# Dense second stage of a PEER layer: gating held one pair of columns ahead, weight tiles of the first stage recorded with priority

## The chip, the cores and the metric

The program runs on one core of a Trainium2 chip. The metric is the device time of one execution in microseconds (us), lower is better. PE is the matrix engine, DVE the vector engine, ACT the scalar engine, POOL the engine that issues indirect gathers, SP the queue that issues all other transfers.

## What is computed

Two stacks of layers follow each other in one program. The change lies in the first stack, in the feed-forward part of its two layers, which picks 128 of 16384 experts for each token and adds their outputs. Cut to what matters:

```python
def peer_ffn(h, wq, subkeys, u, v):
    ...                                   # scores, two top-16, cand, top-16 of cand
    gate = jax.nn.softmax(top, axis=-1)
    def block(args):
        hk, ek, gk = args
        act = jax.nn.gelu(jnp.einsum('ted,td->te', u[ek], hk), approximate=False)
        return jnp.einsum('te,ted->td', gk * act, v[ek])
```

The second stack (fox, gla, gdn and gated feed-forward layers) is not touched.

## The kernel before

`peer` (from L909) runs once in each of the two layers, `l` = 0 and 1. Layer 0 has 512 tokens: 128 of them fetch their experts by gathers (`fetched`, L895 and L900 on DVE, L899 on POOL), the other 384 take the dense way. In layer 1 all 256 tokens are dense. The dense way multiplies every token with every expert and lets the gates, zero for most, choose. The 16384 experts are 128 columns of 128.

The first stage makes the activations. `ahead` (L968) takes one column: `load_w` (L277) loads its weights (`wraw`, 512 KB), ACT rounds them into `whi` (L217), DVE takes the rest into `wlo` (L284), PE runs 24 matmuls (L982), ACT applies gelu into `ev`, and every second column a store puts two columns into the DRAM tensor `u` (L987). Beside it `route` works out the gates: top-16 searches on DVE (`choose`), then `spread`, whose step makes one-hot rows of four tokens (`oa` L836, `ob` L845 in layer 1), multiplies them (PE, L849), and ACT lays the result out for a store into the DRAM tensor `g` (L855). Columns are called from between the steps of `route` by a plan of costs (`tp`, `td`); what is left runs behind it.

The second stage goes over the 128 columns in pairs. `load_u` (L1019) brings four columns of `u` into a tile `ad`, `load_g` (L1012) eight columns of `g` into `gt`, `load_v` (L1024) one column's value rows into `vr`. `gated` (L1029) multiplies a pair's activations by its gates (two DVE multiplications, L1038) and splits the product into `wt`: the rounded half on ACT, the rest on DVE (L294). `products` (L1042) splits a column's `vr` into `whi` (ACT) and `wlo` (DVE, L294) and runs its matmuls (L1054): 18 in layer 0, 12 in layer 1, the last third of which need `wlo`. Buffers: two for `ad`, two for `gt`, three for `wt`, five (layer 0) or six (layer 1) for `vr`, two for `wlo` in layer 0 and three in layer 1.

The program writes the instructions down in the order of the Python code; a scheduler at build time then orders each engine's queue by priority (earlier written comes first, unless raised by `high_priority`), by when it thinks data and buffers are there, and by edges that the kernel adds itself. One such edge is made by `behind` (L204): it puts an instruction behind the last one noted in `self.last` for its engine, which for DVE is the last rest-half of `load_w` or `split` that was written down. Each engine then runs its queue in that fixed order.

Of the kernel before, what the change touches and what calls it, by code (L numbers as in the profile page):

```python
# [52 lines left out]
         dict(nbig=2048, bufs=0, w=(6, 0, 0), mm=2, sm=6, sp=6, uv=4, H=1, acc=1))  # L53
ROUTE = (dict(bufs=7, rt=1, VI=1, t=3, r=13, alt=1, oa=3, ob=2, ev=2),
         dict(bufs=5, rt=1, VI=1, t=3, r=13, alt=2, oa=3, ob=2, ev=4, xw=1, whi=2, wlo=2))
DENSE = (dict(bufs=0, gt=2, ad=2, wt=3, vr=5, o=2, jk=1), dict(bufs=0, gt=2, ad=2, wt=3, vr=6, whi=3, wlo=3, o=2))

LAST = 8
KEEP = dict(xhl=2, nq=3, na=1, nr=2)
WORK2 = (dict(bufs=3, tn=L2, t=14, er=1, g0=2, qg=1, kl=8, hh=16, qs=8, vn=4, p=4, pT=4, o=9, mm=3, sm=1, S=2, PT=1, PO=1),  # L60
         dict(bufs=7, tn=L2, t=7, m=6, at=4, lv=2, o=6, y=5, mm=2, sm=1, A=5),
         dict(bufs=6, tn=L2, t=4, p=3, ce=5, el=1, mt=1, lq=4, DT=4, DTm=1, NL=4, NLm=1, XT=4, XTm=1, aT=4, aTm=1, dl=5,
              o=4, r=6, mm=2, sm=2, A=4),
# [23 lines left out]
class Kern:  # L87
# [171 lines left out]
    def t(self, n=None, dt=F32, tag="t"):  # L259
        if tag in KEEP:  # L260
            return self.keep.tile([P, n or self.tn], dt, name=tag, bufs=KEEP[tag])
        pool = self.lower_tmp if tag in self.lower_tags else self.tmp
        return pool.tile([P, n or self.tn], dt, name=tag, bufs=self.tags[tag])
# [645 lines left out]
    def peer(self, l, extra=()):  # L909
        nc, A, x = self.nc, self.A, self.x  # L910
# [32 lines left out]
        def fetch_for(us, every):  # L943

            nonlocal fd
            n = 0
            if steps:
                fd += us
                while fd >= every:
                    fd -= every  # L950
                    n += next(steps[0], 1) is None
            return n
# [15 lines left out]
        def ahead():  # L968
            nonlocal early
            j = early  # L970
            early += 1
            ps = self.ps("MM")[:, :ND]
            if whole:
                raw = self.w.tile([P, 1024], F32, name="wraw", bufs=self.wb[0])
                nc.sync.dma_start(raw, A["uT"][l, j])
                terms = [(raw[:, k * P:(k + 1) * P], xw[:, k]) for k in range(KD)]
            else:
                hi, lo = self.load_w(A["uT"][l, j])
                terms = [(hi[:, k * P:(k + 1) * P], z[k, dc]) for k in range(KD) for z in (xh, xl)]
                terms += [(lo[:, k * P:(k + 1) * P], xh[k, dc]) for k in range(KD)]  # L980
            for i, (w_, x_) in enumerate(terms):
                nc.tensor.matmul(ps, w_, x_, start=i == 0, stop=i == len(terms) - 1)  # L982
            if j % 2 == 0:
                pair.append(self.t(2 * ND, tag="ev").rearrange("p (j t) -> p j t", j=2))
            self.last["ACT"] = self.actv(pair[-1][:, j % 2], ps, AF.Gelu).ins
            if j % 2:
                nc.sync.dma_start(U[:, j - 1:j + 1], pair.pop())  # L987

        done = 0
        for pe, dve in self.route(l, xh, xl, cs, G, F, fetch):  # L990
            n = fetch_for(dve, EVERY[l])
            done += n
            tp, td = tp + pe, td + dve + n * 2.55
            while tp < td and early < P - LAST:
                ahead()
                tp, td = tp + ND * CU[l], td + (0.0 if whole else 1.1)
        while early < P:
            ahead()
            done += fetch_for(ND * CU[l], 10.0)
        routing.close()  # L1000
        self.part(dense, **DENSE[l])
        left = F - done
# [5 lines left out]
        J, JU, JG = 2, 4, 8  # L1008
        gts, ads, raws = {}, {}, {}
        b3 = lambda z: z.rearrange("p (b t) -> p b t", t=GT)  # L1010

        def load_g(n):  # L1012
            if n < P // JG:
                gt = self.t(JG * ND, tag="gt")
                gts[n] = gt.rearrange("p (b j t) -> p j b t", j=JG, t=GT)
                nc.sync.dma_start(gt.rearrange("p (b j) -> p b j", b=nb),
                                  G[:, :nb, n * JG:(n + 1) * JG].rearrange("p b j t -> p b (j t)"))

        def load_u(n):  # L1019
            if n < P // JU:  # L1020
                ads[n] = self.t(JU * ND, tag="ad").rearrange("p (j t) -> p j t", j=JU)
                nc.sync.dma_start(ads[n], U[:, n * JU:(n + 1) * JU])
# [6 lines left out]
        def gated(j0):  # L1029

            if j0 % JG == 0:
                load_g(j0 // JG + 1)
            if j0 % JU == 0:
                load_u(j0 // JU + 1)
            wt = self.t(J * 2 * ND, F32R, "wt").rearrange("p (j s t) -> p j s t", j=J, s=2)
            a = ads[j0 // JU][:, j0 % JU:j0 % JU + J]
            for jj in range(J):
                nc.vector.tensor_mul(b3(a[:, jj]), b3(a[:, jj]), gts[j0 // JG][:, j0 % JG + jj])  # L1038
            self.split(a, wt[:, :, 0], wt[:, :, 1])
            return wt  # L1040

# [23 lines left out]

        VR = DENSE[l]["vr"] - 1
        load_g(0)
        load_u(0)
        for j in range(VR):
            load_v(j)  # L1070
        prev = None
        for j0 in range(0, P, J):
            w = gated(j0)
            if prev is not None:
                products(*prev)
                if j0 % 8:
                    next(extra, None)
                fetch_for(left, P // J - 1)
            prev = (j0, w)
# [30 lines left out]
        for c in range(nd):  # L1110
            o = self.t(D, tag="o")
# [928 lines left out]
```

## Time and profile before

| what | us |
|---|---|
| three runs | 4589.56, 4605.82, 4605.38 |
| their median | 4605.38 |
| the profiled execution | 4596.78 |
| its span, first to last instruction | 4595.0 |
| PE busy in it | 4333.2 (94%) |
| DVE busy | 3382.9 (74%) |
| ACT busy | 2288.5 (50%) |

In that execution the first stage of layer 0 lies between about 387 and 1205 us, its second stage between 1222.7 and 1789.6; the first stage of layer 1 lies between about 2010 and 2558, its second stage between 2569.7 and 2925. Bracketed times in a row of a timeline are the idle time of the engine just before the instruction and what ended it. A busy PE is not a PE at its peak, as its matmuls are pipelined: the number of matmuls in a stretch and the granted clock beside it say more.

### The profile page before, as it was taken

To read this page: it belongs to the slowest core of one execution; us is meant where nothing else is said; L and a number is where in the kernel's file an instruction comes from. 1 tells how busy PE (TensorE), PEld (TensorE's weight loads), DVE (VectorE), ACT (ScalarE), POOL (GpSimd) and SP (SyncE) were. 2 spreads that over 40 slices of the span, in tenths; PEclk is the share of its full clock that TensorE was granted. 3 is DMA by queue.
4 is the path that set the end of the run, shared out by engine and by line. 5 is a ranking of instruction groups with operands and counts; after the bars stand their busy time and mean duration, and the time that the engine had idled before them with its cause. 6 is when DMAs were issued, how large, how long until landed. Compare 5 with 4: busy or idle time off the path is not lost. (4 is left out here: it accounts for less than half of the span.)

```text
span 4595.0 us, 71892 instructions
## 1 busy us (share of the span) xinstructions
PE 4333.2 (94%) x27588; PEld 3934.9 (86%) x27588; DVE 3382.9 (74%) x6338; ACT 2288.5 (50%) x4316; POOL 207.6 (5%) x136
## 2 busy tenths in 40 slices
PE   6999799899899999989999899999999999999999
PEld 5887799899787777889899787779988988899899
DVE  9986998888587667989954566676576576656765
ACT  4443246477333334554544444575445454445753
POOL 0000012222111110000000000000000000000000
PEclk8999899999999999999999999999999998999999
DMA  5423388889898774465577888425544552155355
GB/s 189 133 64 105 113 307 328 318 306 337 306 371 298 277 280 150 146 189 183 195 250 228 273 282 282 140 81 150 173 120 134 172 152 69 52 174 154 92 171 173
DMA packets 262505, 909.39 MB, mean 198 GB/s; under 512 B 26112, under 2 KB 68992, under 8 KB 240016
## 3 DMA queue, kind: packets, MB, share of 16 engines
q1 hardware_dynamic: 243728, 770.57, 51.5%
q0 software_dynamic: 18432, 134.23, 8.0%
q8 instruction: 216, 3.54, 0.3%
q14 instruction: 129, 1.06, 0.1%
HBM read 819.49 MB, written 84.93 MB: 197 GB/s over the span
## 5 line engine op out<-in xcount | busy, mean ns | idle before, releaser
L217 ACT ACTIVATE whi<-wraw 128x1024 fp32r<-128x1024 f32 (+2 forms) x796 | 831.9, 1046 | 995.6 <-PE MM L307 545.7
L284 DVE TENSOR_TENSOR wlo<-wraw,whi 128x1024 fp32r<-128x1024 f32 (+2 forms) x796 | 957.3, 1204 | 289.8 <-ACT whi L217 167.6
L307 PE MATMUL MM<-xhl,whi 128*128 128x272 f32 (+1 forms) x4736 | 938.8, 295 | 6.9 <-ACT whi L217 6.4
L307 PE MATMUL MM<-b,whi 128*128 128x272 f32 (+2 forms) x3712 | 855.7, 324 | 59.2 <-ACT b L217 50.6
L307 PEld LDWEIGHTS MM<-xhl,whi 128*128 128x128 f32 x4736 | 754.7, 191 | 28.1 <-issue 10.3
L307 PEld LDWEIGHTS MM<-b,whi 128*128 128x128 f32 x3712 | 624.5, 193 | 114.4 <-ACT b L217 56.6
L307 PE MATMUL MM<-xhl,wlo 128*128 128x272 f32 (+1 forms) x2368 | 691.2, 292 | 2.2 <-DVE wlo L284 2.1
L982 PE MATMUL MM<-b,whi 128*128 128x384 f32 (+1 forms) x4096 | 676.8, 315 | 7.4 <-ACT ev L217 7.4
L1054 PE MATMUL SM<-whi,wt 128*128 128x512 f32 x2560 | 632.0, 394 | 30.8 <-ACT whi L217 30.5
L982 PEld LDWEIGHTS MM<-b,whi 128*128 128x128 f32 x4096 | 624.8, 193 | 9.7 <-ACT ev L217 8.8
L1054 PEld LDWEIGHTS SM<-whi,wt 128*128 128x128 f32 x2560 | 487.6, 191 | 135.2 <-ACT whi L217 31.6
L307 PE MATMUL MM<-b,wlo 128*128 128x272 f32 (+2 forms) x1856 | 598.4, 324 | 5.2 <-DVE wlo L284 4.6
L307 PEld LDWEIGHTS MM<-xhl,wlo 128*128 128x128 f32 x2368 | 451.6, 191 | 10.2 <-issue 4.7
L217 ACT ACTIVATE whi<-vr 128x1024 fp32r<-128x1024 f32 x256 | 271.0, 1059 | 366.4 <-PE SM L1054 309.1
L307 PEld LDWEIGHTS MM<-b,wlo 128*128 128x128 f32 x1856 | 356.4, 192 | 30.7 <-DVE wlo L284 9.9
L982 PE MATMUL MM<-b,wlo 128*128 128x384 f32 (+1 forms) x2048 | 348.5, 313 | 28.6 <-DVE wlo L284 28.6
L1054 PE MATMUL SM<-wlo,wt 128*128 128x512 f32 x1280 | 342.5, 399 | 27.3 <-DVE wlo L294 27.0
L294 DVE TENSOR_TENSOR wlo<-vr,whi 128x1024 fp32r<-128x1024 f32 x256 | 310.4, 1222 | 65.3 <-ACT whi L217 50.3
L982 PEld LDWEIGHTS MM<-b,wlo 128*128 128x128 f32 x2048 | 314.1, 191 | 33.8 <-DVE wlo L284 33.2
L1054 PEld LDWEIGHTS SM<-wlo,wt 128*128 128x128 f32 x1280 | 243.2, 192 | 86.6 <-DVE wlo L294 36.9
L1038 DVE TENSOR_TENSOR ad<-ad,gt 128x384 f32<-128x384 f32 (+1 forms) x256 | 112.8, 488 | 221.5 <-DMA ad<-u 185.7
L899 POOL DMA_INDIRECT uv<-uv,sp x128 | 206.6, 1614 | 1517.0 <-DVE acc L895 907.6
(473 smaller groups left out, 5125.3 us busy)
## 6 DMA issues: line engine op xcount, KB each, us to landing
wraw<-uT SPq DMA_DIRECT2D x256, 512.0 KB, 4.6
vr<-uv SPq DMA_DIRECT2D x256, 512.0 KB, 7.0
wraw<-w_gate_up SPq DMA_DIRECT2D x176, 512.0 KB, 3.6
g<-b SPq DMA_DIRECT2D x40, 1024.0 KB, 9.0
wraw<-w_in SPq DMA_DIRECT2D x64, 512.0 KB, 3.8
wraw<-fox_w_in SPq DMA_DIRECT2D x64, 512.0 KB, 3.6
wraw<-w_down SPq DMA_DIRECT2D x64, 512.0 KB, 3.5
wmod<-wmodT SPq DMA_DIRECT2D x56, 512.0 KB, 3.8
```

The lines of the kernel that those rows point to most:

```text
L217: r = nc.scalar.activation(out, in_, func, **kw)
L284: self.last["DVE"] = nc.vector.tensor_sub(lo[:, :n], raw[:, :n], hi[:, :n].bitcast(F32)).ins
L294: self.last["DVE"] = self.nc.vector.tensor_sub(lo, src, hi.bitcast(F32)).ins
L307: nc.tensor.matmul(ps, w_, x_[k, slice(a, b)], start=(i == 0 and q == 0), stop=(i == kc - 1 and q == 2))
L899: nc.gpsimd.indirect_dma_start(z, None, self.A[f"uv{l}"], bass.IndirectOffsetOnAxis(ap=ids[:, js], axis=0))
L982: nc.tensor.matmul(ps, w_, x_, start=i == 0, stop=i == len(terms) - 1)
L1038: nc.vector.tensor_mul(b3(a[:, jj]), b3(a[:, jj]), gts[j0 // JG][:, j0 % JG + jj])
L1054: nc.tensor.matmul(res[c][h], wt[:, jj, s_, c * P:(c + 1) * P], v[:, h * 512:(h + 1) * 512], start=first and q == 0 and s_ == 0, stop=end ...
```

## The change

Four edits: the multiplications of `gated` get the edge of `behind`; in layer 1 `ad` gets a third buffer and `load_u` runs two tiles ahead instead of one (two before the loop, in front of the first `vr`); and `load_w` in the first stage is written down with priority, in both layers (both have more than 192 dense tokens).

```diff
-DENSE = (dict(bufs=0, gt=2, ad=2, wt=3, vr=5, o=2, jk=1), dict(bufs=0, gt=2, ad=2, wt=3, vr=6, whi=3, wlo=3, o=2))
+DENSE = (dict(bufs=0, gt=2, ad=2, wt=3, vr=5, o=2, jk=1), dict(bufs=0, gt=2, ad=3, wt=3, vr=6, whi=3, wlo=3, o=2))
...
+AHEAD = (1, 2)
...
-                hi, lo = self.load_w(A["uT"][l, j])
+                with self.tc.high_priority():
+                    hi, lo = self.load_w(A["uT"][l, j])
...
-                load_u(j0 // JU + 1)
+                load_u(j0 // JU + AHEAD[l])
...
-                nc.vector.tensor_mul(b3(a[:, jj]), b3(a[:, jj]), gts[j0 // JG][:, j0 % JG + jj])
+                self.behind(nc.vector.tensor_mul(b3(a[:, jj]), b3(a[:, jj]), gts[j0 // JG][:, j0 % JG + jj]), "DVE")
...
-        load_u(0)
+        for n in range(AHEAD[l]):
+            load_u(n)
```

No instruction is added or taken away on any engine, and the order of POOL stays as it was. Everything behind layer 1's second stage keeps its order. Lines of the changed kernel are two to four higher than those of before.

DVE in layer 0's second stage, around the gating of the tile `ad_13026`. Before:

```order
L294 TENSOR_TENSOR wt_12967<-ad_12788,wt_12967 128x2x384
L895 SCALAR_TENSOR_TENSOR acc_2891<-uv_12961,sp_4381,acc_2891 128x1024
L294 TENSOR_TENSOR wlo_12975<-vr_12856,whi_12974 128x1024
L1038 TENSOR_TENSOR ad_13026<-ad_13026,gt_12904 128x384 x2
L294 TENSOR_TENSOR wlo_12999<-vr_12880,whi_12998 128x1024
L900 SCALAR_TENSOR_TENSOR uv_13020,sp_4380<-uv_13020,H_4341 128x1024
L294 TENSOR_TENSOR wt_13028<-ad_12906,wt_13028 128x2x384
L1038 TENSOR_TENSOR ad_13026<-ad_13026,gt_12904 128x384 x2
L294 TENSOR_TENSOR wlo_13036<-vr_12913,whi_13035 128x1024
```

The same tile in the changed kernel:

```order
L902 SCALAR_TENSOR_TENSOR uv_13020,sp_4380<-uv_13020,H_4341 128x1024
L1041 TENSOR_TENSOR ad_12906<-ad_12906,gt_12666 128x384 x2
L897 SCALAR_TENSOR_TENSOR acc_2891<-uv_13020,sp_4381,acc_2891 128x1024
L296 TENSOR_TENSOR wlo_13036<-vr_12913,whi_13035 128x1024
L296 TENSOR_TENSOR wt_13028<-ad_12906,wt_13028 128x2x384
L296 TENSOR_TENSOR wlo_13060<-vr_12937,whi_13059 128x1024
L1041 TENSOR_TENSOR ad_12906<-ad_12906,gt_12666 128x384 x2
L296 TENSOR_TENSOR wt_13081<-ad_12906,wt_13081 128x2x384
L296 TENSOR_TENSOR wlo_13089<-vr_12972,whi_13088 128x1024
L296 TENSOR_TENSOR wlo_13113<-vr_12996,whi_13112 128x1024
L902 SCALAR_TENSOR_TENSOR uv_13134,sp_4380<-uv_13134,H_4341 128x1024
L1041 TENSOR_TENSOR ad_13026<-ad_13026,gt_12904 128x384 x2
```

The first gating of `ad_13026` stood in front of `wlo_12999`; it now stands behind `wlo_13113`, which is five columns later (12999, 13036, 13060, 13089, 13113). Its buffer is that of `ad_12788`, which is free once `wt_12967` is written. Counted over the 64 pairs of layer 0, a pair's gating stood 5 to 9 columns ahead of the column it belongs to for 55 of them; now it stands 2 columns ahead for 62. In layer 1 it stood 3 to 7 columns ahead for 56 pairs and now stands 2 ahead for 63.

SP at the start of layer 1's second stage. Before:

```order
L1016 DMA gt<-g_66 128x8x256
L1022 DMA ad<-u_68 128x1024
L1027 DMA vr<-uv 128x1024 x5
L1016 DMA gt<-g_66 128x8x256
L1022 DMA ad<-u_68 128x1024
```

In the changed kernel:

```order
L1019 DMA gt<-g_66 128x8x256
L1025 DMA ad<-u_68 128x1024 x2
L1030 DMA vr<-uv 128x1024 x5
L1019 DMA gt<-g_66 128x8x256
L1025 DMA ad<-u_68 128x1024
```

A second tile of `u` (512 KB) is asked for ahead of the five `vr`. From the third tile on, an `ad` load stands nine columns ahead of its gating in the changed layer 1; in the changed layer 0 it stands five columns ahead (counted as above, against the `vr` load in front of it).

DVE at the end of `spread` in layer 1, before:

```order
L845 TENSOR_SCALAR ob<-iotaf,rt 128x128 x4
L836 TENSOR_TENSOR oa<-iotaf,rt 128x512
L845 TENSOR_SCALAR ob<-iotaf,rt 128x128 x4
L284 TENSOR_TENSOR wlo<-wraw,whi 128x1024
L836 TENSOR_TENSOR oa<-iotaf,rt 128x512
L845 TENSOR_SCALAR ob<-iotaf,rt 128x128 x4
L836 TENSOR_TENSOR oa<-iotaf,rt 128x512
L845 TENSOR_SCALAR ob<-iotaf,rt 128x128 x4
L836 TENSOR_TENSOR oa<-iotaf,rt 128x512
L845 TENSOR_SCALAR ob<-iotaf,rt 128x128 x4
L284 TENSOR_TENSOR wlo<-wraw,whi 128x1024 x82
```

In the changed kernel:

```order
L847 TENSOR_SCALAR ob<-iotaf,rt 128x128
L286 TENSOR_TENSOR wlo<-wraw,whi 128x1024
L847 TENSOR_SCALAR ob<-iotaf,rt 128x128 x3
L838 TENSOR_TENSOR oa<-iotaf,rt 128x512
L847 TENSOR_SCALAR ob<-iotaf,rt 128x128 x4
L838 TENSOR_TENSOR oa<-iotaf,rt 128x512
L847 TENSOR_SCALAR ob<-iotaf,rt 128x128 x2
L286 TENSOR_TENSOR wlo<-wraw,whi 128x1024
L847 TENSOR_SCALAR ob<-iotaf,rt 128x128 x2
L838 TENSOR_TENSOR oa<-iotaf,rt 128x512
L847 TENSOR_SCALAR ob<-iotaf,rt 128x128 x4
L286 TENSOR_TENSOR wlo<-wraw,whi 128x1024 x66
```

Weight tiles stood one to five or six steps of `spread` and now stand one to two or three; 16 tiles fewer are left behind it. In layer 0 the number of tiles in front of each landmark of the routing moves by two at most.

## Rows read from the trace of the kernel before

**Rows 1.** Windows, L1054 alone: PE busy (matmuls), weight loads, granted clock, DMA share, GB/s.

```profile
1222.70:1480.00 257.30, 246.16 (x1043) 201.37 (x1044) 0.96 0.92 334
1480.00:1670.00 190.00, 174.95 (x735) 142.11 (x735) 0.95 0.78 275
1670.00:1790.00 120.00, 119.79 (x529) 98.91 (x527) 1.00 0.63 217
2569.70:2925.00 355.30, 353.88 (x1536) 288.45 (x1536) 1.00 0.83 279
```

**Rows 2.** Timeline of PE, layer 0's second stage: start, duration, instructions, [idle before].

```profile
1222.71 5.49 PE L1054 MATMUL SM<-whi,wt 128*128 128x512 f32 x12 [19.23 <-ACT whi L217]
...
1313.09 2.88 PE L1054 MATMUL SM<-whi,wt 128*128 128x512 f32 x12
...
1317.17 2.88 PE L1054 MATMUL SM<-whi,wt 128*128 128x512 f32 x12
...
1789.63 1.95 PE L1091 MATMUL MM<-ident,acc 128*128 128x128 f32 x16
```

**Rows 3.** Waits of PE, 1222 to 1800: us in total, times, longest.

```profile
PE SM L1054 <- DVE wlo L294: 26.2, 10, 4.5
```

**Rows 4.** Timelines of SP, DVE and PE around the longest of these waits.

```profile
1537.68 0.33 SPq L1022 DMA_DIRECT2D ad<-u  x1
...
1550.11 1.03 DVE L1038 TENSOR_TENSOR ad<-ad,gt 128x384 f32<-128x384 f32 x2 [10.12 <-DMA ad<-u]
1551.06 1.22 DVE L294 TENSOR_TENSOR wlo<-vr,whi 128x1024 fp32r<-128x1024 f32 x1
...
1544.91 2.88 PE L1054 MATMUL SM<-whi,wt 128*128 128x512 f32 x12
1552.33 2.86 PE L1054 MATMUL SM<-wlo,wt 128*128 128x512 f32 x6 [4.54 <-DVE wlo L294]
```

**Rows 5.** Waits of DVE, 1222 to 1800.

```profile
DVE ad L1038 <- DMA ad<-u: 87.5, 19, 10.1
```

**Rows 6.** Page, costliest groups: busy, mean ns, then idle before and its releasers.

```profile
L1038 DVE TENSOR_TENSOR ad<-ad,gt 128x384 f32<-128x384 f32 (+1 forms) x256 | 112.8, 488 | 221.5 <-DMA ad<-u 185.7
```

**Rows 7.** Windows, all engines, first stage of layer 1 (the last is its tail).

```profile
2110.00:2222.00 112.00, 107.69 (x872) 105.08 (x870) 111.98 (x237) 57.01 (x89) 0.00 (x0) 1.00 0.61 191
2222.00:2330.00 108.00, 95.20 (x730) 89.69 (x729) 107.20 (x294) 54.35 (x142) 0.00 (x0) 1.00 0.57 212
2330.00:2558.00 228.00, 228.00 (x1902) 228.00 (x1901) 95.60 (x78) 105.11 (x157) 0.00 (x0) 1.00 0.72 224
```

**Rows 8.** Instructions on the tile ad, both layers: transfer, issue to landing.

```profile
DMA to landing us min/median/max: 4.3/8.3/20.8
```

**Rows 9.** Windows, all engines (PE, PEld, DVE, ACT, POOL), layer 0's second stage.

```profile
1260.00:1290.00 30.00, 30.00 (x134) 24.82 (x134) 28.25 (x40) 12.09 (x18) 6.17 (x3) 1.00 1.02 388
1310.00:1400.00 90.00, 90.00 (x399) 74.54 (x398) 75.71 (x102) 35.58 (x48) 12.49 (x8) 1.00 0.93 343
```

**Rows 10.** Timelines of DVE, ACT and PE, start of layer 1's second stage.

```profile
2566.55 1.43 DVE L1038 TENSOR_TENSOR ad<-ad,gt 128x256 f32<-128x256 f32 x4 [12.50 <-DMA ad<-u]
...
2568.61 1.04 ACT L217 ACTIVATE whi<-vr 128x1024 fp32r<-128x1024 f32 x1
...
2569.70 3.63 PE L1054 MATMUL SM<-whi,wt 128*128 128x512 f32 x8 [11.29 <-ACT whi L217]
```

**Rows 11.** Groups by form, 1670 to 1790: the two halves of wt.

```profile
L294 DVE TENSOR_TENSOR wt<-ad,wt 128x768 fp32r<-128x768 f32 x12 | 11.5, 955 | 0.0
...
L217 ACT ACTIVATE wt<-ad 128x768 fp32r<-128x768 f32 x12 | 10.2, 847 | 3.3 <-PE SM L1054 3.3
```

**Rows 12.** Groups by form, 2222 to 2320.

```profile
L284 DVE TENSOR_TENSOR wlo<-wraw,whi 128x1024 fp32r<-128x1024 f32 x10 | 12.6, 1255 | 0.0
```

**Rows 13.** First stage of layer 0: window 387 to 1205, and one PE wait.

```profile
387.00:1205.00 818.00, 756.95 (x4367) 727.54 (x4365) 704.24 (x1467) 442.32 (x1088) 139.97 (x90) 0.96 0.74 268
...
PE MM L880 <- DVE sp L931: 6.8, 1, 6.8
```

## Prediction

> **What bounds the kernel now.** PE is busy for 94% of the span, so I looked for the stretches where it stands still or runs slowly, and asked which of them the edits can reach. I read the windows of the two second stages first, then PE's waits, then the timelines around the longest one, and last the windows of the first stages.
>
> In layer 1's second stage PE is busy for 353.88 of 355.30 us at full clock [rows 1]: nothing to win but its start. Layer 0's second stage is another matter. At full clock one column takes 4.08 us, from 1313.09 to 1317.17 [rows 2], so 128 columns want 522.2 us. From the first matmul at 1222.71 to the first one behind the stage at 1789.63 it took 566.9 [rows 2]: 44.7 too many. PE's waits name 26.2 of them, ten waits for `wlo` [rows 3]. The other 18.5 are matmuls at the lower of the two clock levels behind a wait and small gaps: the granted clock is 0.96 and 0.95 in the first two stretches against 1.00 in the third [rows 1], and after the 4.54 us wait six matmuls took 2.86 us where 1.4 is usual (a third of 4.08) [rows 2, 4].
>
> Why is `wlo` late? Rows 4 show it. SP asks for a tile of `u` at 1537.68; DVE sits idle for 10.12 us until it lands, does the gating at 1550.11 and only then, at 1551.06, the `wlo` that PE has wanted since about 1547.8. That `wlo` needs nothing of the tile; it merely stands behind the gating. DVE lost 87.5 us in 19 such waits in this stage [rows 5]; over both layers `ad` ended 185.7 us of idle time in front of the gating [rows 6].
>
> In the first stage of layer 1 DVE is the bound of `spread`: 107.20 of 108 us busy from 2222 to 2330, while PE has 95.20 [rows 7]. Behind it PE runs alone at full rate, 228.00 of 228 [rows 7].
>
> **The change, term by term.** No instruction comes or goes, so every term is idle PE time, or slow PE time, won or lost.
>
> Gating, layer 0. In the example the tile's gating moves five columns later, behind five `wlo`s. At 4.08 us each the load then has about 20 us from its issue, plus what stood between before, against a landing of 8.3 us in the median and 20.8 at most [rows 8]. So nearly all waits for `ad` leave DVE, and those of PE for `wlo` with them. The hold doesn't delay the load: the buffer is freed by the last `wt` of the tile two earlier, which moves back with its own gating, but so does the use. What can be won is 44.7 less the slow start, 12 matmuls in 5.49 us where 2.88 is usual [rows 2], so 42.1. By stretches: 1043 matmuls are 57.9 columns or 236.4 us against 257.3, 18.3 to win without the start; 735 are 166.6 against 190.0, 23.4 to win; 529 are 119.9 against 120.0, nothing [rows 1].
>
> Not all of the first stretch is to be had, since its transfers get denser. It moved 334 GB/s for 257.3 us, 85.9 MB [rows 1]; in 239 us (236.4 and the slow start) that is 359 GB/s. The trace shows PE fully busy at 343 GB/s for 90 us, with the DMA engines at 0.93, and at 388 for 30 us, with them at 1.02 [rows 9]. If 343 is all that lasts, the stretch takes 250.5 us and 6.8 are won; at 388 nothing binds and 18.3 are won. I take 14, nearer to the upper end, because at 343 the engines were not full. In the second stretch 52.3 MB in 166.6 us are 314 GB/s, below both, and I take 21 of 23.4, leaving something for a tile that lands very late. Together **35 us won**, bounds 25 and 42.
>
> The Trainium skill ("DMA: Bandwidth & Descriptors", Specifications) gives an HBM limit of about 358 GB/s per core, half of what its stack gives two. By it the first stretch would take 85.9/358, 240 us, and 17.3 would be won in place of my 14. The trace passes that figure, 388 for 30 us [rows 9], so I keep to the rows.
>
> Gating, layer 1. PE has no waits to lose here, and the hold leaves a tile nine columns of 2.77 us (355.30/128 [rows 1]), 25 us, between load and gating, more than the longest landing. Zero, covered by that lead. With the cover gone each late tile would cost what it lacks.
>
> Start of layer 1's second stage. PE's first matmul waits for `whi` on ACT, which stands behind both halves of two pairs' `wt` [rows 10]. Before, all four gatings went first, in 1.43 us; now the second pair's stand behind a `wt` on DVE, which delays ACT's second `wt` and so `whi` by about 1.4 us (an ACT half and a DVE half of `wt`, together 1.8 in the wider layer 0 [rows 11], less what overlaps). The extra tile of `u` adds 512 KB ahead of the first `vr`, at 343 GB/s 1.5 us, side by side with this. **1.5 us lost**, bounds 0 and 3. At the start of layer 0's stage SP's order is unchanged: zero.
>
> Priority of the weight tiles, layer 1. In `spread` 15 more tiles are worked on (43 against 28 from the second top-16 search on), and they leave the tail. A tile is 24 matmuls, in the tail 228.00/1902 x 24 = 2.88 us [rows 7], and 1.26 us of DVE [rows 12]. `Spread` then takes DVE 107 + 19 = 126 us and PE 95 + 43 = 138: PE becomes its bound, and its 12.8 us of idle time are covered. From 2110 to 2222 another 4.3 are idle [rows 7]. I take **10 us won** of 17.1, as the fixed order of DVE still makes PE wait here and there; bounds 0 and 17. What is late next is nothing: the last store of `g` moves back some 30 us and still lies far ahead of the second stage.
>
> Priority, layer 0. PE has 61 us of idle time in 387 to 1205 [rows 13], but the tiles in front of each landmark hardly move, and PE's order still ends at points that DVE sets, as the 6.8 us in front of `sp` [rows 13]. A `wlo` that comes sooner lets PE wait longer at the next such point. **1 us won**, bounds -6 and 8.
>
> The sum is -35 + 1.5 - 10 - 1 = -44.5 against the profiled execution's 4596.78: **4552 us**. That execution lies 8.6 below the median of the three runs, 7.2 above the lowest and 9.0 below the highest. 0.5%, about what a measurement of this kernel can tell from no change, is 23 us.
>
> **The rivals.**
> *The DMA engines are the bound* in more than the first stretch: tiles of `vr` and gathers take over as the late ones once `u` no longer is. For it: shares of 0.92 in the first stretch and above 1 for 30 us [rows 1, 9]. Against it: 0.78 and 0.63 later, and layer 1's stage runs full at 279 GB/s [rows 1]. It gives 7 of the first stretch and 6 of the second, and 5 in layer 1's `spread`: 18 less, 4579.
>
> *The order changes but nothing comes of it*: DVE waits as long at other places, or PE simply arrives earlier at points that others set. For it: the DVE of the first stretch is 94% busy for 30 us [rows 9]. It gives 4596, give or take 8.
>
> *The hold is too tight, and the kernel gets slower.* `Wt` now has two columns, 8.16 us, to be made, and DVE still has splits, gathers' products and modulation rows in between. If DVE can't fit a pair's work into 8.16 us, the chain of two gatings, ACT's half and DVE's half, 2 x 0.49 + 0.85 + 0.95 = 2.8 us [rows 6, 11], lies bare: 29 pairs of the first stretch make 81 us, less 31 from elsewhere, 4647. It decides from the point where a pair costs DVE more than 8.16. Against it: at full PE rate it cost 75.71/90 x 8.16 = 6.9 for 90 us, 7.7 in the densest 30 [rows 9].
>
> **How the numbers follow.** The forecast has 0.62, the DMA bound 0.20, no effect 0.11, slower 0.07. The forecast's own terms reach from 4530 (-42 + 0 - 17 - 8 = -67) to 4581 (-25 + 3 + 0 + 6 = -16); the first rival, 4579, lies inside, and the runs spread by some 8 around the profiled one. Leaving out the slower case, and the part of no effect above 4590, gives 4527 to 4590, with 3 us at the bottom for that spread. Faster by over 0.5% means below 4582: nearly all of the forecast and half of the first rival, 0.71. Within 0.5%: 0.21. Slower: 0.08.
>
> **What would show it.** In the changed profile layer 0's second stage should last about 532 us in place of 566.9, PE's waits there for `wlo` fall from 26.2 to under 6, DVE's waits for `ad` from 87.5 to under 15, and the clock of the first two stretches reach 0.98. The DMA share of the first stretch should rise to about 0.97. From `spread` to the end of layer 1's first stage PE should lose 10 us of idle time, with a shorter tail, and the start of its second stage should take 1 to 2 us more. I would be wrong if DVE waits as long for `vr` or gathers in place of `ad`, or if PE waits for `wt`.

## The result, and the profile after

The changed kernel takes 4521.77 us in the median of six runs (4518.53 to 4530.46); the kernel before took 4604.8 beside it. The ratio is 0.9825, 95% interval 0.9807 to 0.9844: 1.75% faster, 83 us. Forecast were 4552 and a range from 4527 to 4590. The direction was right, the size about half of what came, and the time lies 5 us below the range. Two executions at a low granted clock (7002.1 us of the kernel before at 0.56, 4767.2 us of the kernel `both` at 0.84) are left out of every median below.

The two profiled executions differ by 78.3 us of span. Four landmarks on PE cut the span into stages; after, they are these rows (timeline of PE, as in [rows 2, 10]):

```profile
1209.31 5.48 PE L1057 MATMUL SM<-whi,wt 128*128 128x512 f32 x12 [20.86 <-ACT whi L219]
...
1734.16 1.95 PE L1095 MATMUL MM<-ident,acc 128*128 128x128 f32 x16
...
2495.54 3.78 PE L1057 MATMUL SM<-whi,wt 128*128 128x512 f32 x8 [12.40 <-ACT whi L219]
...
2846.78 2.05 PE L1095 MATMUL MM<-ident,o 128*128 128x128 f32 x16
```

With the first activation matmul (at 387.1 before, 387.0 after) and the landmarks of before (1222.71, 1789.63, 2569.70, 2925.11) they give the stages. A is layer 0's first stage, from its first activation matmul to the first matmul of the second stage; B is layer 0's second stage; C reaches from its end to the first matmul of layer 1's second stage; D is that stage; the rest is the second stack.

| stage | before | after | change | forecast (bounds) |
|---|---|---|---|---|
| A | 835.6 | 822.3 | -13.3 | -1 (-8 to 6) |
| B | 566.9 | 524.9 | -42.0 | -35 (-42 to -25) |
| C | 780.1 | 761.4 | -18.7 | -10 (-17 to 0), with part of the start's 1.5 |
| D | 355.4 | 351.2 | -4.2 | rest of the start's 1.5 |
| rest | 1669.9 | 1669.9 | 0.0 | 0 |

The 18.7 us of C are not all the change's: 3.2 of them lie between the end of B and layer 1's first activation matmul (2039.64 before, 1980.98 after). That stretch took 246.8 to 252.1 us in all fourteen profiles of this document, with no order among the kernels, so below C is also given from that matmul on.

In stage B the waits are gone that the argument was about. Who PE waited for, 1205 to 1735, in place of the ten waits of [rows 3] one line, and that one is the start of the stage:

```profile
PE SM L1057 <- ACT whi L219: 20.9, 1, 20.9
```

Who DVE waited for, 1209 to 1735; the line for `ad` [rows 5] is gone:

```profile
DVE wlo L296 <- ACT whi L219: 51.3, 36, 2.6
DVE wlo L296 <- PE SM L1057: 34.0, 12, 2.9
DVE wt L296 <- ACT wt L219: 11.8, 12, 1.2
```

DVE now waits for the rounding of its own column and for PE to give a `wlo` buffer back: it is ahead of PE, not behind it. The tile's load has the lead that the prediction worked out. In the timelines of SP and DVE, at about the place of [rows 4], 20.2 us lie between asking and gating, and the gating has no idle time in front of it:

```profile
1536.95 0.33 SPq L1025 DMA_DIRECT2D ad<-u  x1
...
1557.19 1.02 DVE L1041 TENSOR_TENSOR ad<-ad,gt 128x384 f32<-128x384 f32 x2
```

The windows of both second stages, L1057 alone (columns as in [rows 1]):

```profile
1209.30:1450.00 240.70, 240.69 (x1051) 199.06 (x1052) 0.99 0.95 355
1450.00:1620.00 170.00, 170.00 (x752) 140.77 (x751) 1.00 0.86 306
1620.00:1734.20 114.20, 114.20 (x505) 94.33 (x503) 1.00 0.64 230
...
2526.00:2626.00 100.00, 100.00 (x443) 82.81 (x442) 1.00 0.92 310
```

1051 matmuls are 58.4 columns, 238.2 us at 4.08, and with the slow start of 2.6 us the stretch is filled to the microsecond. So is the second: 752 are 41.8 columns, 170.5. Nothing of B is left to win but its start.

The one group row of the gating over both layers, against [rows 6]: idle time 27.6 in place of 221.5 us, all of it in two waits at the starts of the second stages.

```profile
L1041 DVE TENSOR_TENSOR ad<-ad,gt 128x384 f32<-128x384 f32 (+1 forms) x256 | 114.2, 485 | 27.6 <-DMA ad<-u 27.6
```

Layer 1's first stage, all engines (PE, PEld, DVE, ACT, POOL), against [rows 7]: `spread` (2140 to 2290) and the tail.

```profile
2140.00:2290.00 150.00, 149.84 (x1235) 147.07 (x1235) 146.70 (x354) 80.25 (x192) 0.00 (x0) 1.00 0.70 237
2290.00:2483.00 193.00, 193.00 (x1610) 192.94 (x1608) 80.86 (x66) 88.16 (x132) 0.00 (x0) 1.00 0.71 220
```

`spread` takes longer, with more columns in it, and now both engines are full: PE 149.84 of 150, DVE 146.70. The tail is shorter, 193 us in place of 228.

### The profile page after: what moved, and what is told of

Read it like the earlier page. It is cut to its first block, busy times and chain, and to the rows that moved or that the text cites. A ratio compares the mean times of both kernels' runs of the same rounds, so it can differ in the third digit from the quotient of the medians.

```text
span 4516.7 us, 71876 instructions
## 1 busy us (share of the span) xinstructions
PE 4296.7 (95%) x27588; PEld 3913.7 (87%) x27588; DVE 3389.9 (75%) x6338; ACT 2280.8 (50%) x4316; POOL 215.6 (5%) x136
## 4 chain that ended last, share of the span: by engine, by line
PE 49%; ACT 2%; DVE 2%; issue 0%; DMA 0%; SPq 0%; ACTq 0%; DVEq 0%
PE MM L309 26%; PE SM L1057 8%; PE MM L985 7%; PE SM L851 1%; PE PO L1383 1%; DVE wlo L286 1%; PE A L1886 1%; PE A L1880 0%; ACT whi L219 0%; PE PT L1377 0%; ACT t L219 0%; ACT hh L219 0%; PE S L1366 0%; PE SM L1319 0%; PE A L513 0%
## 5 line engine op out<-in xcount | busy, mean ns | idle before, releaser
L1057 PE MATMUL SM<-whi,wt 128*128 128x512 f32 x2560 | 626.5, 391 | 33.3 <-ACT whi L219 33.3
L1057 PEld LDWEIGHTS SM<-whi,wt 128*128 128x128 f32 x2560 | 483.4, 189 | 134.5 <-ACT whi L219 33.8
L1057 PE MATMUL SM<-wlo,wt 128*128 128x512 f32 x1280 | 332.6, 390 | 0.0
L1057 PEld LDWEIGHTS SM<-wlo,wt 128*128 128x128 f32 x1280 | 241.0, 188 | 50.3
L851 PE MATMUL SM<-ob,oa 128*128 128x128 f32 x1280 | 188.0, 286 | 23.3 <-ACT ob L219 23.0
```

Source lines behind the costliest of these rows:

```text
L851: nc.tensor.matmul(pg[:, ts], ohs[0][:, ts], b_[:, ts], start=True, stop=True)
L1057: nc.tensor.matmul(res[c][h], wt[:, jj, s_, c * P:(c + 1) * P], v[:, h * 512:(h + 1) * 512], start=first and q == 0 and s_ == 0, stop=end ...
```

## The experiments

Each time below is the median of the kernel's runs, four of most, ten of ahead and ad3, beside the median of the kernel before on the same chip (4609.1 for gate, prio, ahead and prio_lo, 4606.3 for after2, prio_ld, hold4 and expl, 4604.2 for the last four). A ratio is estimated from the runs of both kernels with its interval; it is not the quotient of the two medians, from which it differs by up to 0.001. The stages come from the landmarks of each kernel's one profile:

| kernel | time | ratio (95%) | A | B | C | D |
|---|---|---|---|---|---|---|
| before | 4604.8 | 1 | 835.6 | 566.9 | 780.1 | 355.4 |
| changed | 4521.8 | 0.9825 (0.9807 to 0.9844) | 822.3 | 524.9 | 761.4 | 351.2 |
| gate | 4550.0 | 0.9868 (0.9848 to 0.9887) | 831.0 | 524.9 | 779.6 | 351.6 |
| prio | 4581.0 | 0.9929 (0.9907 to 0.9952) | 820.3 | 575.4 | 762.9 | 361.1 |
| ahead | 4606.2 | 0.9995 (0.9983 to 1.0007) | 831.0 | 574.2 | 779.7 | 357.9 |
| prio_lo | 4530.2 | 0.9821 (0.9800 to 0.9842) | 830.0 | 524.0 | 764.9 | 350.7 |
| after2 | 4526.8 | 0.9818 (0.9797 to 0.9839) | 827.4 | 524.1 | 764.4 | 351.0 |
| prio_ld | 4547.6 | 0.9869 (0.9846 to 0.9892) | 834.8 | 525.3 | 778.9 | 351.2 |
| hold4 | 4520.1 | 0.9807 (0.9786 to 0.9828) | 823.9 | 523.8 | 762.9 | 350.8 |
| expl | 4512.3 | 0.9786 (0.9764 to 0.9807) | 822.7 | 524.6 | 758.3 | 350.9 |
| lo0 | 4542.1 | 0.9870 (0.9854 to 0.9887) | 823.7 | 525.1 | 779.6 | 350.8 |
| ad3 | 4619.5 | 1.0027 (1.0014 to 1.0041) | 832.5 | 579.7 | 779.8 | 358.1 |
| both | 4518.3 | 0.9806 (0.9786 to 0.9826) | 825.4 | 524.3 | 761.1 | 351.1 |
| head25 | 4510.9 | 0.9799 (0.9783 to 0.9816) | 818.2 | 525.1 | 755.6 | 350.9 |

**The edits one by one.** gate is the kernel before with the first edit, prio with the second, ahead with the third alone:

```diff
+self.behind(nc.vector.tensor_mul(...), "DVE")          # gate
+with self.tc.high_priority():                          # prio
+    hi, lo = self.load_w(A["uT"][l, j])
+dict(..., ad=3, ...); AHEAD = (1, 2)                   # ahead
```

Expected of gate:

> Kernel before plus the edge of `behind` on the gating, nothing else. Stage lengths by PE's landmarks in the kernel before: first stage of layer 0 (387.1 to its first L1054) 835.6 us, second 566.9, first stage of layer 1 (to its first L1054) 780.1, second 355.4; in the changed kernel 822.2, 524.9, 761.4, 351.2. Theory: the edge alone ends DVE's waits for u tiles in both second stages, so layer 0's takes 525 +- 2, layer 1's 351 to 353, the first stages stay at 835.6 and 780.1 within 1, and the total falls by 45 (4551 by profile). Rival: the order of the first stages also prepares the second (less backlog of gathers and transfers when it starts), and the edge alone leaves layer 0's second stage at 540 or more, the total 20 to 30 lower.

Measured: B 524.9 and D 351.6 by the edge alone, C unchanged, 59.1 us less in the median. The theory holds; A's 831.0 is not the edge's doing, as ahead shows the same with the order of before. The median moved by more than the stages (42.0 + 3.8 + 4.6). One reason is that the profiled execution of before was one of its faster ones: prio and ahead, which have its order in stage B, show 575.4 and 574.2 there where it shows 566.9.

Expected of prio:

> Kernel before plus priority for load_w in the first stages, nothing else. Theory: the priority alone makes the first stages 822 and 761 us (from 835.6 and 780.1), the second stages stay at 566.9 and 355.4 within 2, the total falls by 32 (4564 by profile). Rival: part of the 13 and 19 us came from the held gating (transfers and buffers of the stage before), and priority alone gives half or less, 4580 or more.

Measured: A 820.3 and C 762.9, as in the changed kernel, and 28.1 us less in the median. B and D are not 566.9 and 355.4 but 575.4 and 361.1; their order is that of before, so this is the spread just named. The first stages' gain is the priority's.

Expected of ahead:

> Kernel before plus the third ad buffer and the u load two tiles ahead in layer 1, nothing else. Theory: in layer 1's second stage a load two tiles ahead also ends DVE's waits for u (98 us, 26 times), so that stage goes from 355.4 to 352 us, its start costs 1 more; everything else stays; total 2 to 4 lower, which the times can't tell from nothing. Rival: the 4 us of layer 1's second stage come from the edge alone; then this kernel shows 355 to 357 there.

Measured: D 357.9, no gain, and the time can't be told from the kernel before. The theory on D falls; D's 4 us are the edge's (gate 351.6; the changed kernel, which has the buffer too, 351.2). The third buffer does nothing here: counted on DVE, the gating stood 3 to 7 columns ahead for 56 of the 64 pairs in before, and stands 8 to 11 ahead for 49 in ahead.

**A buffer instead of the edge.** ad3 gives layer 0 what ahead gave layer 1:

```diff
-DENSE = (dict(bufs=0, gt=2, ad=2, ...
+DENSE = (dict(bufs=0, gt=2, ad=3, ...
+AHEAD = (2, 1)
```

> Kernel before, with a third u buffer in layer 0 and its load two tiles ahead, no edge and no priority. Theory: a gating that is tied to nothing runs forward with its load (that is what the order shows), so DVE still waits for u tiles and the needed wlo behind them: layer 0's second stage 565 to 577 as in three profiles without the edge (566.9, 575.3, 574.2), total that of the kernel before within 8. Rival: what was missing is a longer lead of the load, and a buffer gives it as well as the edge: 525 to 540, total 35 to 50 lower.

Measured: B 579.7, and the kernel is slower than before by 0.27% (0.14 to 0.41). Waits of DVE and of PE in B, 1210 to 1785:

```profile
DVE ad L1039 <- DMA ad<-u: 146.5, 26, 13.6
```
```profile
PE SM L1055 <- DVE wlo L295: 34.6, 18, 4.8
```

With one more buffer DVE waits for `ad` 133 us past the start of the stage (13.6 of the 146.5 are the wait at the start) and PE 34.6 for `wlo`. In before these are 87.5 [rows 5] and 26.2 [rows 3], in prio 103.3 and 32.0, in ahead 100.2 and 32.6, all three with the old order of B. So the buffer cures nothing, and costs a little. The reason can be counted on DVE: the gating stood 5 to 9 columns ahead for 55 of the 64 pairs, and now stands 9 to 13 columns ahead for 55. The earlier load took the gating forward with it, as the theory says. So what cured stage B is the tie of the gating to the columns.

**How far ahead.** hold4 holds the gating behind a split that was written down two columns sooner:

```diff
+self.splits.append(self.last["DVE"])                   # in split
-self.behind(nc.vector.tensor_mul(...), "DVE")
+self.after(r.ins, self.splits[-4])                     # taken ahead of the wt split; from the fourth pair on
```

> Changed kernel, but a pair's gating is held behind a split that was written down two columns sooner (four columns ahead of its own instead of two). Theory: what counts is the lead of the u load before its gating; it falls from about five columns to three in layer 0 (12 us against a landing of 8.3 in the median, 20.8 at most), so DVE's waits for u come back in part, 10 to 40 us, PE's for wlo a few us, and layer 0's second stage takes 527 to 540 instead of 525; layer 1 (nine to seven columns) stays at 351 to 352. Rival: any edge that ties the gating to the columns does it, the lead is of no matter: 525 again.

Measured: B 523.8, the time that of the changed kernel. In the order that came of it the gating stands three or four columns ahead, for 58 of the 64 pairs. The lead of the load fell less than the theory had it, from 20 us in the median to 16: the load starts when the `wt` two tiles before is written, so if the gating moves, the load moves with it, as the prediction had said and this expectation forgot. The shortest lead, past the first two tiles, is 11.4 us, and DVE waited for `ad` only twice there, 2.5 us in all; past the start of the stage PE did not wait at all.

**Which of the three instructions of `load_w`.** prio_lo and prio_ld are the changed kernel with only DVE's rest half raised, or only the transfer and ACT's half; lo0 raises the rest half in layer 0 alone:

```diff
-with self.tc.high_priority():
-    hi, lo = self.load_w(A["uT"][l, j])
+hi, lo = self.load_w(A["uT"][l, j], ("lo",))           # prio_lo; prio_ld: ("load", "hi"); lo0: () if l else ("lo",)
```

> Changed kernel, but of the three instructions of load_w only DVE's rest half (wlo) is written down with priority; transfer and ACT's half are not. Theory: what counts is where DVE does wlo among the route's work (in the changed kernel one every 4 us around 870 to 890, before none from 870.5 to 885.8 and then two): then the first stages are 822 +- 4 and 761 +- 4 and the total is that of the changed kernel within 8. Rival: an earlier transfer and an earlier rounding on ACT are what counts: then the first stages are those of the kernel before (835, 780) and the total is 30 above the changed kernel.

> Changed kernel, but of the three instructions of load_w only the transfer and ACT's rounded half are written down with priority, DVE's rest half is not. With the rest half alone raised, the first stage of layer 1 went to 764.8 (of 780 to 761), that of layer 0 stayed at 830.0. Theory 1: in layer 1 all of the gain hangs on wlo, so this kernel shows 778 to 781 there; in layer 0 the 7.75 us wait near 887 us comes back, and the stage takes 829 or more. Theory 2: in layer 0 it is the earlier transfer and ACT's half that make the gain; then that stage takes 820 to 825 here.

> Changed kernel, but in layer 0 only DVE's rest half of load_w is raised, and in layer 1 nothing is. First stage of layer 0 so far: raised in full 822.3, 827.4, 820.3, 823.9; not raised 835.6, 831.0, 831.0; transfer and ACT half raised 834.8; rest half raised 830.0 in its one profile. Theory: the rest half gives what the full priority gives, and the 830.0 was the spread of one profile: then 819 to 828 here, layer 1's first stage 779 to 781, total 4541 +- 5. Rival: it takes all three instructions: then 829 to 834 again, total 4549 +- 5, as with the gating edge alone.

Measured: in C the rest half is all of it (prio_lo 764.9, prio_ld 778.9, with lo0 back at 779.6). In A the waits say so too. PE's three waits for `wlo` there, 20.0 us in before, are gone in prio_lo and lo0, and with transfer and ACT's half raised they are back; the longest but one is 4.06 in place of 7.75:

```profile
PE MM L988 <- DVE wlo L290: 16.3, 3, 10.6
```

How much of A's time hangs on the rest half is less clear. prio_lo and lo0, which have one and the same order on DVE in A, took 830.0 (outside the 826 expected) and 823.7 there. Four profiles with all three raised (changed, after2, prio, hold4) took 820.3 to 827.4, 823.5 in the mean; five with the rest half unraised (before, gate, ahead, ad3, prio_ld) took 831.0 to 835.6, 833.0 in the mean. The full priority is thus worth 8 to 10 us in A, and 15 to 17 in C from the first activation matmul on (530.0 to 531.8 unraised, 513.0 to 515.4 raised). The rest half alone, with a mean of 826.9, gives most of it in A; whether the other two instructions give the rest or it is the spread of single profiles is open. The times don't decide it: lo0 lies 62.1 us under the kernel before on its chip, gate 59.1 and prio_ld 58.7 on theirs, at ratios of 0.9870, 0.9868 and 0.9869.

The same kernel again:

> The changed kernel once more, beside the next three. Stage lengths in its first profile: first stage of layer 0 822.3, second 524.9, first stage of layer 1 761.4, second 351.3. Three kernels with an unraised first stage of layer 0 gave 835.6, 831.0 and 831.0 there, so that stage differs by some 5 from one profile to the next. If the 822.3 is the order's doing, this profile shows 819 to 826 again; if it was chance, 828 or more.

It gave 827.4, between the two. By the means above the gain isn't chance, but part of the 13.3 us of the first pair of profiles was.

**The next wait of the same kind.** In the changed kernel PE's longest wait inside stage A is 18.42 us, ended by ACT's gelu, which stands behind the softmax's Exp, which waits for DVE. expl writes that Exp down later, both adds hold4's edge, head25 also calls five more columns ahead of the first gates:

```diff
-self.actv(g, g, AF.Exp)
 for p in range(2):
+    if p == 1:
+        self.actv(g, g, AF.Exp)
...
-HEAD = (10.0, 0.0)
+HEAD = (25.0, 0.0)                                     # head25 alone
```

> Changed kernel, with the softmax's Exp of a token tile written down one step of the route later (behind the first of the two one-hot sums). In the changed kernel ACT sits 16.55 us in front of that Exp (at 539.4 us), and PE 18.42 us in front of the matmuls whose gelu stands behind it. Theory: PE's wait there falls under 6 us and the first stage of layer 0 gets 8 to 15 us shorter (808 to 815), layer 1's by 0 to 5. Rival: PE stands still at the next point that DVE sets (the 7.89 us in front of sp grow to 20), and nothing is won.

> Changed kernel with the two edits that did no harm: Exp one step of the route later, and the gating held four columns ahead instead of two. Theory: the 5 to 6 us that the later Exp took off layer 1's first stage (514.3 and 514.5 to 507.8 from its first activation matmul on) come again, layer 0's second stage stays at 524, total 4505 to 4515. Rival: that gain was chance, and the total is that of the changed kernel, 4520 to 4527.

> The kernel of the run before, with five more columns of layer 0 called ahead of the first gates (14 instead of 9 in front of the transposes that wait for sp; the plan's start value 25 instead of 10). With the later Exp PE stood still for 27.8 us there, so the wait had only moved. Theory: PE does five columns of 4.16 us in that wait, so 21 of the 27.8 us go, DVE's chain to sp gets 6 us longer by five rest halves of 1.2, and the first stage of layer 0 falls by 10 to 15 to about 810, the total to 4495 to 4505. Rival: DVE sets the length of the stage up to the one-hot rows; what PE does sooner it lacks later, and the stage stays at 820 to 827 or grows by DVE's 6 us.

Timeline of PE at that place, in the changed kernel, then expl, then head25:

```profile
541.58 4.92 PE L985 MATMUL MM<-b,whi 128*128 128x384 f32 x16 [18.42 <-ACT ev L219]
...
559.94 2.16 PE L882 MATMUL MM<-ident,r 128*128 128x128 f32 x8 [7.89 <-DVE sp L933]
```
```profile
559.62 2.17 PE L883 MATMUL MM<-ident,r 128*128 128x128 f32 x8 [27.80 <-DVE sp L934]
```
```profile
577.68 2.17 PE L884 MATMUL MM<-ident,r 128*128 128x128 f32 x8 [24.66 <-DVE sp L935]
```

In layer 0 the wait moved whole to the next point that DVE sets (18.42 + 7.89 against 27.80), as the rival said. In layer 1 PE's 6.2 us wait for `ev` went. From the first activation matmul on C took 507.8, 509.0 and 507.5 us in expl, both and head25, against 513.0 to 515.4 in the five kernels with priority there and the Exp where it was: some 6 us that came all three times.

expl's four runs (4508.9 to 4518.3) lie below all of after2's beside it (4525.0 to 4528.9), by 14 us in the median. Not all of that is the Exp's: hold4's four on the same chip (4514.3 to 4522.7) lie below after2's as well, and the profiled execution of expl spans 4516.6 us, that of the changed kernel 4516.7. both has 4518.3, outside what was expected. So past the 6 us in layer 1, what the later Exp gives is open. head25 moved the point at which the gates are ready 18 us back without filling the wait, yet has the shortest A, 818.2, and 4510.9: not the forecast 4495 to 4505, and not to be told from expl.

## Why the prediction was wrong

The sum said 44.5 us; the two profiles show 78.2 in the four stages. The 33.7 that are missing are 12.3 in A, 8.7 in C, 7.0 in B and 5.7 in D. Two steps failed. In layer 0's first stage I counted the weight tiles in front of each landmark and put the term at 1 us; it is 8 to 10. In both stages of layer 1 I took a busy PE for a PE at its rate, and so left out time that no list of waits shows. The gating in layer 0 was only mis-sized.

**Gating, layer 0: right in mechanism, mis-sized.** DVE's waits, PE's waits and the lead came as described. Two sizes were off. "I take 14" of 18.3, for denser transfers: all of it came. PE was busy for 240.69 of 240.70 us at 355 GB/s and a DMA share of 0.95, so the density that "If 343 is all that lasts" feared was no bound. And 21 of 23.4 was all of 23.4. The term is 42, not 35. Also, the profiled execution that the sum was made against was fast in just this stage (566.9 against 575.4 and 574.2 of the same order), so against those two the edge was worth some 50.

**Gating and start, layer 1.** The step that failed here is "nothing to win but its start". A column there takes 2.72 us, as two rows of the changed kernel's PE show:

```profile
2503.89 1.98 PE L1057 MATMUL SM<-whi,wt 128*128 128x512 f32 x8
...
2506.61 1.98 PE L1057 MATMUL SM<-whi,wt 128*128 128x512 f32 x8
```

That is 348.2 us for 128, not the 355.3 that I divided by. Of the 7 us between, 1.7 are the slow first column and 1.4 idle time [rows 1]; the rest shows in no list of PE's waits, only in the count: 353.88 of 355.30 was a busy PE, not one at its rate. All that is lost behind the first column lies in fifteen columns that took 0.2 to 0.8 us too long each. I had counted columns in layer 0 and read a share in layer 1. DVE's waits (2565 to 2926, before) were there to see, as in layer 0:

```profile
DVE ad L1038 <- DMA ad<-u: 98.2, 26, 12.5
```

After, no wait for `ad` is left past the start, and every column from the third on but the last takes 2.72 us. The start itself cost 2.3 us, 1.1 in the wait for `whi` and 1.2 in the first two columns, inside its bounds.

**Priority, layer 1: the size came, but not from where I took it.** From the first activation matmul on C fell from 530.1 to 514.6, near the upper bound of 17. "I take 10 us won of 17.1, as the fixed order of DVE still makes PE wait here and there" was nearly right for the idle time. Waits of PE in that stretch (up to the start of the second stage), before:

```profile
PE MM L982 <- DVE wlo L284: 8.5, 12, 1.5
PE SM L849 <- DVE ob L845: 6.9, 18, 0.5
PE MM L982 <- ACT ev L217: 1.6, 3, 0.6
```

After:

```profile
PE MM L985 <- ACT ev L219: 6.2, 1, 6.2
PE MM L985 <- DVE wlo L286: 1.3, 1, 1.3
```

17.0 us became 7.5, since one new wait for ACT took the place of thirty small ones for DVE. The other 7 us are busy time, as the windows of the same stretch show, before and after (all engines):

```profile
2039.60:2569.00 529.40, 501.54 (x4038) 489.96 (x4037) 383.16 (x900) 253.85 (x453) 0.00 (x0) 0.99 0.64 208
...
1981.00:2494.60 513.60, 494.30 (x4038) 487.68 (x4037) 383.77 (x900) 248.97 (x452) 0.00 (x0) 0.98 0.67 215
```

The same 4038 matmuls kept PE busy 501.5 us and now 494.3, and the granted clock isn't the reason. It repeats: 501.5 to 502.3 in the six kernels whose rest halves are not raised in layer 1 (before, gate, ahead, ad3, lo0, prio_ld), 494.1 to 494.4 in the five where they are and the Exp is in its old place. It shows in `spread`: from 2222 to 2330 each of 730 matmuls took 0.130 us of busy time, against 0.120 in the tail [rows 7], though 453 of them are the short ones of L849. In the changed kernel, from 2140 to 2290 and with 512 short ones, it is 0.121. What slowed them before is open, as no row names a wait for it. That the term came near its upper bound was thus luck in part: the bound counted idle time alone.

**Priority, layer 0: the step that was wrong.** "The tiles in front of each landmark hardly move", and so 1 us. The count was right and was the wrong thing to count. Between two landmarks the same `wlo`s can stand in a bunch or spread out. Timelines of DVE and PE, 869 to 888, before:

```profile
869.25 1.22 DVE L284 TENSOR_TENSOR wlo<-wraw,whi 128x1024 fp32r<-128x1024 f32 x1
...
885.79 2.35 DVE L284 TENSOR_TENSOR wlo<-wraw,whi 128x1024 fp32r<-128x1024 f32 x2
...
887.07 4.51 PE L982 MATMUL MM<-b,wlo 128*128 128x384 f32 x16 [7.75 <-DVE wlo L284]
```

After, DVE:

```profile
869.21 1.21 DVE L286 TENSOR_TENSOR wlo<-wraw,whi 128x1024 fp32r<-128x1024 f32 x1
...
873.74 1.21 DVE L286 TENSOR_TENSOR wlo<-wraw,whi 128x1024 fp32r<-128x1024 f32 x1
...
878.49 1.21 DVE L286 TENSOR_TENSOR wlo<-wraw,whi 128x1024 fp32r<-128x1024 f32 x1
...
882.14 1.16 DVE L286 TENSOR_TENSOR wlo<-wraw,whi 128x1024 fp32r<-128x1024 f32 x1
...
886.82 1.21 DVE L286 TENSOR_TENSOR wlo<-wraw,whi 128x1024 fp32r<-128x1024 f32 x1
```

Before, DVE does 15 us of routing between two `wlo`s, and PE, which wants one every 4.16 us, stands still for 7.75. After, they come every 4 to 5 us. prio_lo, lo0 and prio_ld show that this wait hangs on DVE's half, not on the transfer. The row of that wait stood in the trace of before, and I had not asked for it. For another wait my reason held: "A `wlo` that comes sooner lets PE wait longer at the next such point". PE's waits in A for the weights, for `ev` and for `sp` (6.8 before [rows 13]), before:

```profile
PE MM L982 <- DVE wlo L284: 20.0, 3, 10.6
PE MM L982 <- ACT ev L217: 5.8, 1, 5.8
```

After:

```profile
PE MM L985 <- ACT ev L219: 18.4, 1, 18.4
PE MM L882 <- DVE sp L933: 7.9, 1, 7.9
```

The longest wait for `wlo`, 10.6 us at about 532, only moved into the 18.4 for `ev`; the 7.75 and a third of 1.6 went for good. All told PE's idle time in A is 72.0 us in the mean of the four profiles with the full priority and 78.2 in that of the five without, 6 us less; busy time is 3 less.

**The range.** The far end of my bounds was 4530, and the terms came near or past their far ends all together (42 of 42 in B, 16 of 17 in C, 8 to 10 of 8 in A), with 4 us of layer 1's second stage outside. The terms of B and C, both cut for the belief that some wait would remain, were not independent. The fast base does not explain the miss: it was fast in B, and the changed kernel's 525 us there do not depend on it.

**The rivals.** The DMA bound is out: PE at full rate at 355 GB/s. The Trainium skill ("DMA: Bandwidth & Descriptors", Specifications) puts the HBM limit at about 358 GB/s per core; the stretch stays just under it in the mean, and 30 us of it (1250 to 1280) moved 401 with PE fully busy, so the trace passes that figure for a while, and no run here shows what would hold for longer. The hold that is too tight is out too: PE never waited for `wt`, and four columns ahead did no better than two.

## What to carry to other kernels

Where each engine runs a fixed queue, an instruction that waits for a transfer is best tied to the work it feeds; a deeper buffer alone let it run forward to the next wait here, and cost 0.27% in one of two kernels. When an order changes, don't count the work in front of landmarks: look for the longest run of other work between two pieces that the slowest engine wants one after the other. And count rate, instructions times their time at full clock, in each stage before writing that nothing is to be won there.

## What the runs showed that was not expected

With the edge, B took 523.8 to 525.3 us in ten profiles; without it 566.9, 575.4 and 574.2 with the same order of the stage. Stage A, which keeps its waits, spread from 820.3 to 827.4 in four profiles of one order on DVE (changed, after2, prio, hold4), from 831.0 to 835.6 in four of another (before, gate, ahead, ad3), and took 830.0 and 823.7 with a third (prio_lo, lo0). Waits alone don't make a stage spread: the first stage of layer 1, from its first activation matmul on, keeps 17 us of them in the old order and took 530.0 to 530.5 in four profiles of it. But a single profile of a stage like A, or like B before, is no base for a sum of a few microseconds.
